# An encoder layer on one core: own buffers for one quarter of x, and another order of products in the first input block

## The chip, the cores and the metric

The kernel runs on one core of one Trainium2 chip. The metric is the device time of one execution in microseconds (us). Below, TensorE is the matrix engine (PE in the profile, PEld its weight loads), VectorE is DVE, ScalarE is ACT, GpSimd is POOL, and SyncE (SP) issues all the DMA transfers spoken of here.

## The reference

One layer of a streaming encoder runs over 2048 prompt tokens and a sample of 8 x 16 tokens, with a model width of 1024. Two groups of heads (an mLSTM with a matrix state, and attention over a sliding window) are fed by one combined input projection. Their results go through an output projection, a LayerNorm, a convolutional feed-forward network and a second LayerNorm. Everything is float32. The part that matters here is the input projection `x @ w_in`:

```python
def trunk_layer(x, pos, C0, n0, m0, k_cache, v_cache, conv_prev, mchunk, w_in, ...):
    qm, km, vm, om, ip, fp, qa, ka, va = split_in(x @ w_in)
    ...
    mix = jnp.concatenate([hm, ha], axis=-1) @ w_out
    h = layer_norm(DEEPNORM_ALPHA * x + mix, ln1_g, ln1_b)
    f, conv_rows = conv_ffn(h, conv_prev, w_up, w_conv, b_conv, w_down)
    y = layer_norm(DEEPNORM_ALPHA * h + f, ln2_g, ln2_b)
```

## The kernel before

**Split numbers.** A float32 operand is split into two parts that TensorE takes: ScalarE casts it to the high half (a 128x1024 cast takes about 1.05 us), VectorE subtracts that from the source and leaves the low half (about 1.2 us). Each product is then three matmuls: high x high, high x low, low x high.

**Blocks and groups.** The input projection goes through four blocks of 512 prompt tokens (`IBLOCKS`; the first block carries the 128 sample tokens as a fifth tile, index 4). In each block five groups g = 0 to 4 of 512 weight columns are computed (g 0 and 1: queries and keys of the mLSTM; 2: queries of the attention; 3 and 4: output gates and values).

**Seven products.** Each group of a block is computed by a scheme of Strassen's kind: x is cut into quarters (xr 1 to 4), the weights too, and seven products s = 1 to 7 of half size replace eight. Product s reads the x combination of the same number. Three PSUM banks A, B, C take them: A takes products 1 and 2; B takes 6, 5 and 3 on top of a copy of A; C takes 7 and 4. `i_after` empties the banks:

- after 6, ScalarE copies B into a tile u2 (L826 calls the copy of L815);
- after 2, A is copied out and stored (`i_out`, L807);
- after 5, ScalarE copies B into u4 (L815) and VectorE adds C to it (L819, or L821 for g of 2 and more); u4 is stored;
- after 4, VectorE adds C to u2 (same lines), and u2 is stored;
- after 3, B is copied out (L807) and refilled with A (L843), where product 1 of the next group stands already.

In the first block the sample's tokens are multiplied along with products 1, 2, 5 and 4 into a bank psx (L758). For g of 0 and 1 they are transposed later (pxt, L875), behind the product that follows 4.

**Direct tiles.** Gates and the keys and values of the attention are not done by the scheme. For each tile of 128 tokens a direct product (item "t", L774) reads two quarters of x as they are. Tiles 0 and 1 of a block read the splits named 1 and 2, tiles 2 and 3 read those named "b12" and 3. The split "b12" is the cast of xr 2, and no product of the scheme reads it. It is written into the buffers of slot 4 (`x_slot(4 if s == "b12" else s)`), which hold the x of product 4 at other times.

**Order.** `i_begin` writes out the order of all items by hand; TensorE runs them in just this order. Block 0 begins with products 1 and 2 of group 0 and 1 of group 1, five direct tiles, then products 7 and 6; then, group by group, 5, 4, 3, 7 and 1 of the next group, 6, 2 and so on. The last group of block 0 ends with 5, 3, 4, and directly behind it come direct tiles 2 and 3 of block 1. In later blocks two direct tiles of the old block stand between the last product and these two. A list `uq` made from the items sets in which order the weights are loaded and split; the splits go through a ring of eight halves, so a split waits until a product has released its buffers. The other engines' instructions and the DMA issues are ordered by a scheduler, by their place in the program and by when it reckons them ready; each engine then works strictly in its order.

**First block's weights.** In block 0 the sums of weight quarters that the scheme needs are made on VectorE in place (`split_first`): for product 7 a11 = a11 - a21 (L528); then a21 = a21 + a22 (L523) and a11 = a22 - a11 (L525), the weight of product 6. For g of 0 and 1 each sum is also stored (`keep`, L521) for the later blocks, and L525 overwrites what the store of product 7's weight reads.

**x's steps.** `x_steps` makes the x combinations: "t3", "t2", "t4", "t1" are VectorE's sums in place (L578, L581, L584, L588), the others are casts (L593 and L594). `begin` says after which item of block 0 the steps of the first block come; `passages` says after which product of a block's last group the steps for the next block come. At the passage from block 0, "b12" comes after product 4. `tc.issue_after(ins)` puts what is issued inside it behind `ins` on the engine of `ins`; it adds no semaphore.

Of the kernel before, what the change touches and what calls it, by code (L numbers as in the profile page):

```python
# [43 lines left out]
NG = 5  # L44
# [160 lines left out]
class Prog:  # L205
# [137 lines left out]
    def i_begin(self):  # L343
        self.ib = [self.dps.tile([P, 512], F32, name="dps", tag="dps") for _ in range(3)]
        it = []
        nb = len(IBLOCKS)
        for b in range(nb):
            if b == 0:
                it += [("p", 0, 0, s) for s in (1, 2)] + [("p", 0, 1, 1)]
                it += [("t", 0, i, -1) for i in (0, 1, 2, 3, 4)] + [("p", 0, 0, s) for s in (7, 6)]  # L350
            else:
                it += [("p", b, 0, s) for s in (1, 7, 6, 2)]
            for g in range(NG):
                if b == 0:

                    it += [("p", b, g, s) for s in (6, 2)] * (g > 0) + [("p", b, g, 5)]
                    if g + 1 < NG:
                        it += [("p", b, g + 1, 1)] * (g > 0) + [("p", b, g, 4), ("p", b, g, 3), ("p", b, g + 1, 7)]
                    else:
                        it += [("p", b, g, 3), ("p", b, g, 4)]  # L360
                elif g + 1 < NG:

                    it += [("p", b, g, s) for s in (6, 7, 2)] * (g > 0)
                    it += [("p", b, g, 5), ("p", b, g + 1, 1), ("p", b, g, 3), ("p", b, g, 4)]
                else:
                    it += [("p", b, g, s) for s in (6, 7, 5, 2, 3, 4)]
            if b:
                it += [("t", b, i, b) for i in (0, 1)]
            if b + 1 < nb:
                it += [("t", b + 1, i, b) for i in (2, 3)]  # L370
        self.items = it

        uq = []
        for i in it:
            if i[0] == "p":
                uq.append(i)
            elif ("g", i[3], 0) not in uq:
                uq += [("g", i[3], u) for u in range(4)]
        uq += [("o", b, h, u) for b in range(len(OBLOCKS)) for h in range(2) for u in range(4)]
        self.uq = uq  # L380
        self.wu, self.hx, self.xr = {}, {}, {}
        self.us = self.ur = 0

        self.halves = [0, 0]
        self.raws = []
        self.raw_of = {}
        self.x_room = {1: [None, False], 7: [None, False]}
        self.xn = self.ny = 0
        self.hs = {}
        self.spare = False  # L390
        self.extra, self.ring, self.turn = None, 2 * WB, 0
        self.raws.append([None, False])
# [177 lines left out]
    def x_steps(self, b, *steps):  # L570

        nc, V = self.nc, self.nc.vector
        r = lambda q: self.xr[b, q]
        for s in steps:
            if s == "t3":
                self.spare = False
                self.xt = e = self.raw_slot([P, 4, HT]) if b else [self.tp.tile([P, 4, HT], F32, name="xt", tag="qk", bufs=2), False]
                V.tensor_sub(e[0], r(4), r(2))  # L578
            elif s == "t2":

                V.tensor_add(self.xt[0], self.xt[0], r(1))  # L581
            elif s == "t4":

                V.tensor_sub(r(4), r(3), self.xt[0])  # L584
                self.xt[1] = True
            elif s == "t1":

                V.tensor_sub(r(2), r(2), r(1))  # L588
            else:
                x = self.xt[0] if s in (7, 6) else r({1: 1, 2: 3, 3: 4, "b12": 2, 5: 2, 4: 4}[s])  # L590

                self.hx[b, s] = h, l = self.x_slot(4 if s == "b12" else s)
                nc.scalar.copy(h, x)  # L593
                V.tensor_sub(l, x, h.bitcast(F32))  # L594

# [17 lines left out]
    def i_dense(self):  # L613
        nc, a = self.nc, self.a
# [17 lines left out]
        for q in (2, 4):  # L632
            for _ in range(2 + (q == 2) * 2):
# [15 lines left out]
                 ("t", 0, 0, -1): ["t2", 6], ("t", 0, 2, -1): ["t1", 5, "t4"]}  # L649
        self.sb, self.trans = {}, None  # L650

        passages = [{1: ["load"], 7: ["t3", 7], 6: ["t2", 6], 3: [3, "t4"], 4: ["b12", "t1"]},
                    {1: ["load"], 6: ["t3"], 7: [7, "t2"], 5: [6], 3: [3, "t4"], 4: ["b12", "t1"]}]
        sums = 0
        after = None
        for item in self.items:
# [9 lines left out]
            if item[0] == "t":  # L666
                _, b, ti, e = item
# [25 lines left out]
            _, b, g, s = item  # L693
# [7 lines left out]
            behind = self.i_after(b, g, s)  # L701
# [4 lines left out]
            if g == last and b + 1 < nb:  # L706
                if s == 7:
                    self.rope_load(IBLOCKS[b + 1][2], 2)
                for x in passages[b > 0].get(s, ()):
                    if x == "load":  # L710
                        self.spare = True
                        self.x_load(b + 1, 1, 2, 3, 4)
                    else:
                        self.x_steps(b + 1, x)
            if (b, g, s) == (0, last, 4):
                self.x_steps(1, 1, 2)
                after = [6, 1]
            if g == last and b + 1 == nb and s in (7, 5, 2, 3):
                self.x_pair(0, (7, 5, 2, 3).index(s))
            with self.tc.issue_after(behind) if behind and b == 0 else nullcontext():  # L720
                self.advance()
                self.x_steps(0, *begin.get(item, ()))
                if item == ("p", 0, 0, 2):
                    self.x_single(4)
# [74 lines left out]
    def i_out(self, b, g, i, j, src):  # L799

        nc = self.nc
        ev = src if i else self.zev()
        if g == 3:
            nc.scalar.activation(ev, src, AF.Tanh, scale=0.5)
            nc.vector.tensor_scalar_add(ev, ev, 1.0)
        elif not i:
            nc.scalar.copy(ev, src)  # L807
        if g == 2:
            self.rope(ev, IBLOCKS[b][2 * j], 2, nc.gpsimd if b > 1 else nc.vector)
        self.i_store(b, g, i, j, ev)  # L810

    def i_after(self, b, g, s):
        nc, V = self.nc, self.nc.vector
        A, B, C = self.ib
        copy = lambda d, x: nc.scalar.activation(d, x, AF.Copy, scale=KSCALE) if g < 2 else nc.scalar.copy(d, x)  # L815

        def add(u):
            if g < 2:
                V.scalar_tensor_tensor(u, C, KSCALE, u, op0=ALU.mult, op1=ALU.add)  # L819
            else:  # L820
                V.tensor_add(u, C, u)  # L821
        if s == 1 and g == 0:
            return nc.scalar.copy(B, A).ins
        elif s == 6:
            self.u2 = self.zev()
            copy(self.u2, B)  # L826
        elif s == 2:
            self.i_out(b, g, 0, 0, A)
        elif s == 5:
            u4 = self.zev()  # L830
            copy(u4, B)
            add(u4)
            self.i_out(b, g, 1, 1, u4)
        elif s == 4:
            add(self.u2)
            self.i_out(b, g, 1, 0, self.u2)
            if b == 0:
                self.i_batch(g)
        elif s == 3:
            self.i_out(b, g, 0, 1, B)  # L840
            if g + 1 < NG:

                nc.scalar.copy(B, A)  # L843
# [1348 lines left out]
```

## Time and profile before

| what | value |
|---|---|
| median of 3 runs | 2310.88 us (2309.37 to 2311.18) |
| the profiled execution | 2311.53 us |
| its span, first to last instruction | 2309.7 us |
| TensorE busy | 2278.2 us (99%) |
| VectorE, ScalarE busy | 1805.2 us (78%), 1305.5 us (57%) |
| DMA moved | 624.98 MB, mean 271 GB/s |
| granted TensorE clock over the span | 0.999 |

The profile tells of one execution. A row of the timeline gives start and duration in us, engine, line of the program, operation, output and inputs, and in brackets how long the engine had been idle and what ended that. A row of the waits gives who waited for whom: us in total, times, longest. A row of the windows gives a stretch, its length, the busy time of PE, PEld, DVE, ACT and POOL in it, the granted TensorE clock, the share of the DMA engines that is busy, and GB/s. A row of the engine groups or DMA issues gives counts and means; for a DMA the KB each and the median us from issue to landing.

### The profile page before, as it was taken

What the parts mean: (1) busy time and instruction counts of PE and PEld (TensorE: products, weight loads), DVE (VectorE), ACT (ScalarE), POOL (GpSimd) and SP (SyncE); (2) the same over time, 40 slices, a digit from 0 to 9 for tenths busy, and PEclk for the clock granted to TensorE, in tenths of its full rate; (3) what the DMA queues carried; (4) which work ended last, traced back from release to release, by engine and by line L of the source; (5) the groups of instructions that cost most, each with busy time, mean ns of one, the idle gap of its engine ahead of it and who ended that gap; (6) DMA issues with size and microseconds to landing.
All of it is one profiled execution on the core that took longest, in us unless ns stands there. A gap on an engine that the chain in (4) does not pass through costs nothing.

```text
span 2309.7 us, 39905 instructions
## 1 busy us (share of the span) xinstructions
PE 2278.2 (99%) x14425; PEld 2099.4 (91%) x14425; DVE 1805.2 (78%) x3157; ACT 1305.5 (57%) x2465; POOL 227.3 (10%) x289
## 2 busy tenths in 40 slices
PE   9999999999999999999999999999999999999998
PEld 8999999999877778999999999999999988888887
DVE  8777587786689888987888667778766787796897
ACT  5453466776766565555556455556555544654653
POOL 0001001001122121200002000002000000000100
PEclk9999999999999999999999999999999999999999
DMA  8898999889976667787777899888998786756753
GB/s 279 300 320 276 302 318 319 293 299 331 302 256 219 219 214 259 272 326 279 281 269 259 278 312 320 311 304 271 331 287 262 243 284 223 244 196 222 245 187 110
DMA packets 297365, 624.98 MB, mean 271 GB/s; under 512 B 47052, under 2 KB 140240, under 8 KB 297168
## 3 DMA queue, kind: packets, MB, share of 16 engines
q1 hardware_dynamic: 296304, 619.29, 78.5%
q10 hardware_dynamic: 864, 3.15, 0.4%
q8 instruction: 114, 1.87, 0.3%
q14 instruction: 83, 0.68, 0.1%
HBM read 451.78 MB, written 170.56 MB: 269 GB/s over the span
## 4 chain that ended last, share of the span: by engine, by line
PE 72%; DVE 6%; DMA 3%; issue 2%; ACT 2%; POOL 0%; SPq 0%; DVEq 0%; ACTq 0%; POOLq 0%
PE dps L1896 18%; PE fup L1896 18%; PE dps L2100 6%; PE dps L749 6%; PE fht L2100 6%; PE fup L2100 5%; PE dps L225 2%; PE dps L227 1%; PE dps L226 1%; PE ppo L1385 1%; PE psc L1336 1%; PE ppt L1379 1%; DVE w L221 1%; DMA wv<-wup 1%; DMA r<-zf 1%
## 5 line engine op out<-in xcount | busy, mean ns | idle before, releaser
L1896 PE MATMUL dps<-hh,uw 128*128 128x384 f32 (+1 forms) x1848 | 477.7, 327 | 5.7 <-DVE u L1929 2.6
L1896 PE MATMUL fup<-hh,uw 128*128 128x384 f32 (+1 forms) x1848 | 476.5, 326 | 0.0
L1944 DVE SCALAR_TENSOR_TENSOR cc<-u,cw,cc 128x768 f32<-128x768 f32 (+1 forms) x264 | 257.6, 977 | 124.9 <-ACT cc L1942 121.5
L1896 PEld LDWEIGHTS dps<-hh,uw 128*128 128x128 f32 x1848 | 329.4, 188 | 8.2 <-DVE u L1929 3.2
L1896 PEld LDWEIGHTS fup<-hh,uw 128*128 128x128 f32 x1848 | 329.4, 188 | 0.0
L1896 PE MATMUL fup<-hl,uw 128*128 128x384 f32 (+1 forms) x924 | 301.3, 326 | 1.0 <-DVE hl L221 1.0
L1896 PE MATMUL dps<-hl,uw 128*128 128x384 f32 (+1 forms) x924 | 301.0, 326 | 0.0
L749 PE MATMUL dps<-w,oh 128*128 128x256 f32 x1344 | 250.2, 282 | 3.6 <-DMA w<-zws 2.1
L749 PEld LDWEIGHTS dps<-w,oh 128*128 128x128 f32 x1344 | 209.2, 188 | 15.9 <-issue 10.5
L220 ACT CAST uw<-wraw 128x1024 fp32r<-128x1024 f32 x126 | 123.2, 981 | 173.4 <-PE dps L2100 104.1
L221 DVE TENSOR_TENSOR w<-wraw,w 128x1024 fp32r<-128x1024 f32 (+1 forms) x155 | 180.8, 1171 | 48.3 <-ACT w L220 46.6
L220 ACT CAST w<-wraw 128x1024 fp32r<-128x1024 f32 (+1 forms) x155 | 155.2, 1008 | 99.8 <-PE dps L749 49.5
L221 DVE TENSOR_TENSOR uw<-wraw,uw 128x1024 fp32r<-128x1024 f32 x126 | 142.4, 1130 | 63.9 <-ACT uw L220 63.8
L749 PE MATMUL dps<-w,ol 128*128 128x256 f32 x672 | 186.2, 277 | 0.0
L1942 ACT ACTIVATE cc<-u,cw 128x768 f32<-128x768 f32 (+1 forms) x132 | 131.9, 999 | 94.6 <-DVE u L1938 91.7
L1896 PEld LDWEIGHTS fup<-hl,uw 128*128 128x128 f32 x924 | 173.5, 188 | 1.8 <-DVE hl L221 1.8
L749 PE MATMUL dps<-oh,w 128*128 128x256 f32 x896 | 170.3, 284 | 4.1 <-ACT zev L807 1.5
L1896 PEld LDWEIGHTS dps<-hl,uw 128*128 128x128 f32 x924 | 173.5, 188 | 0.0
L2100 PE MATMUL fup<-uw,fu 128*128 128x512 f32 x726 | 169.1, 389 | 0.0
L2100 PEld LDWEIGHTS fup<-uw,fu 128*128 128x128 f32 x726 | 136.1, 188 | 28.4 <-ACT fht L2107 0.2
L2100 PE MATMUL dps<-uw,fu 128*128 128x512 f32 x660 | 160.9, 389 | 0.1
L749 PEld LDWEIGHTS dps<-oh,w 128*128 128x128 f32 x896 | 140.4, 188 | 10.4 <-issue 4.1
(346 smaller groups left out, 4596.2 us busy)
## 6 DMA issues: line engine op xcount, KB each, us to landing
uw<-zw SPq DMA_DIRECT2D x176, 512.0 KB, 5.0
zw<-uw SPq DMA_DIRECT2D x88, 512.0 KB, 2.9
w<-zws SPq DMA_DIRECT2D x72, 512.0 KB, 6.2
wv<-wup SPq DMA_DIRECT2D x66, 512.0 KB, 5.8
wraw<-wi SPq DMA_DIRECT2D x62, 512.0 KB, 5.3
wraw<-zt SPq DMA_DIRECT2D x60, 512.0 KB, 4.3
wraw<-wdn SPq DMA_DIRECT2D x45, 512.0 KB, 3.8
wraw<-wo SPq DMA_DIRECT2D x40, 512.0 KB, 4.7
```

The source lines that it names most:

```text
L220: nc.scalar.copy(hi, src)
L221: nc.vector.tensor_sub(lo, src, hi.bitcast(F32))
L225: mm(out, ah, bh, start=start, stop=False)
L226: mm(out, ah, bl, start=False, stop=False)
L227: mm(out, al, bh, start=False, stop=stop)
L749: mm(o, l, r, start=s in (1, 7) and c == k == i == 0, stop=k == 3 and i == 2, skip_group_check=True)
L1336: nc.tensor.matmul(ps[kvh][:, j, :nk], q[rs, j0 + j], k[rs, sel], start=i == 0, stop=i == 2)
L1379: nc.tensor.transpose(pp[:, j * P:(j + 1) * P], scs[j // 2][:, 2 * kvh + j % 2, kt * P:(kt + 1) * P], self.ident)
L1896: mm(ps, l[:, k], r[:, k], start=s in (1, 7) and k == 0 and i == 0, stop=k == 3 and i == 2, skip_group_check=True)
L1942: S.activation(c[:, v], u[:, v, 2:2 + n], AF.Identity, bias=w[3], scale=w[2])
L1944: V.scalar_tensor_tensor(c[:, v], u[:, v, i:i + n], w[i], c[:, v], op0=ALU.mult, op1=ALU.add)
L2100: mm(ps, l[:, k, c], r[:, k], start=s in (1, 4, 7) and u == 0 and k == 0 and i == 0, stop=u == nu - 1 and k == n - 1 and i == 2, skip_grou ...
```

## The change

1. The split "b12" gets two buffers of its own (4 KB per partition each) in place of those of slot 4.
2. At the passage from block 0 to block 1 its cast comes after product 2 of the last group instead of after product 4, and is tied behind the eviction of that product on ScalarE (`i_out` and `i_after` now return that instruction; the tie that existed behind product 1 keeps to product 1).
3. In block 0, group 0 runs 6, 7, 5, 3, 4 instead of 7, 6, 5, 4, 3, and group 1 runs 6, 7, 2 instead of 7 (behind group 0's product 3), 6, 2. The weights of both groups are still split 7 before 6; those of group 0's products 3 and 4 swap with their products.

```diff
--- before.py
+++ after.py
@@ -347,15 +347,17 @@
         for b in range(nb):
             if b == 0:
                 it += [("p", 0, 0, s) for s in (1, 2)] + [("p", 0, 1, 1)]
-                it += [("t", 0, i, -1) for i in (0, 1, 2, 3, 4)] + [("p", 0, 0, s) for s in (7, 6)]
+                it += [("t", 0, i, -1) for i in (0, 1, 2, 3, 4)] + [("p", 0, 0, s) for s in (6, 7)]
             else:
                 it += [("p", b, 0, s) for s in (1, 7, 6, 2)]
             for g in range(NG):
                 if b == 0:
 
-                    it += [("p", b, g, s) for s in (6, 2)] * (g > 0) + [("p", b, g, 5)]
-                    if g + 1 < NG:
-                        it += [("p", b, g + 1, 1)] * (g > 0) + [("p", b, g, 4), ("p", b, g, 3), ("p", b, g + 1, 7)]
+                    it += [("p", b, g, s) for s in ((), (6, 7, 2), (6, 2))[min(g, 2)]] + [("p", b, g, 5)]
+                    if g == 0:
+                        it += [("p", b, g, 3), ("p", b, g, 4)]
+                    elif g + 1 < NG:
+                        it += [("p", b, g + 1, 1), ("p", b, g, 4), ("p", b, g, 3), ("p", b, g + 1, 7)]
                     else:
                         it += [("p", b, g, 3), ("p", b, g, 4)]
                 elif g + 1 < NG:
@@ -376,6 +378,9 @@
                 uq.append(i)
             elif ("g", i[3], 0) not in uq:
                 uq += [("g", i[3], u) for u in range(4)]
+        for g in (0, 1):
+            i, j = [uq.index(("p", 0, g, s)) for s in (6, 7)]
+            uq[i], uq[j] = uq[j], uq[i]
         uq += [("o", b, h, u) for b in range(len(OBLOCKS)) for h in range(2) for u in range(4)]
         self.uq = uq
         self.wu, self.hx, self.xr = {}, {}, {}
@@ -589,7 +594,7 @@
             else:
                 x = self.xt[0] if s in (7, 6) else r({1: 1, 2: 3, 3: 4, "b12": 2, 5: 2, 4: 4}[s])
 
-                self.hx[b, s] = h, l = self.x_slot(4 if s == "b12" else s)
+                self.hx[b, s] = h, l = self.x_slot(s)
                 nc.scalar.copy(h, x)
                 V.tensor_sub(l, x, h.bitcast(F32))
 
@@ -649,7 +654,7 @@
                  ("t", 0, 0, -1): ["t2", 6], ("t", 0, 2, -1): ["t1", 5, "t4"]}
         self.sb, self.trans = {}, None
 
-        passages = [{1: ["load"], 7: ["t3", 7], 6: ["t2", 6], 3: [3, "t4"], 4: ["b12", "t1"]},
+        passages = [{1: ["load"], 7: ["t3", 7], 6: ["t2", 6], 2: ["b12"], 3: [3, "t4"], 4: ["t1"]},
                     {1: ["load"], 6: ["t3"], 7: [7, "t2"], 5: [6], 3: [3, "t4"], 4: ["b12", "t1"]}]
         sums = 0
         after = None
@@ -711,13 +716,14 @@
                         self.spare = True
                         self.x_load(b + 1, 1, 2, 3, 4)
                     else:
-                        self.x_steps(b + 1, x)
+                        with self.tc.issue_after(behind) if x == "b12" and s == 2 else nullcontext():
+                            self.x_steps(b + 1, x)
             if (b, g, s) == (0, last, 4):
                 self.x_steps(1, 1, 2)
                 after = [6, 1]
             if g == last and b + 1 == nb and s in (7, 5, 2, 3):
                 self.x_pair(0, (7, 5, 2, 3).index(s))
-            with self.tc.issue_after(behind) if behind and b == 0 else nullcontext():
+            with self.tc.issue_after(behind) if behind and b == 0 and s == 1 else nullcontext():
                 self.advance()
                 self.x_steps(0, *begin.get(item, ()))
                 if item == ("p", 0, 0, 2):
@@ -800,14 +806,16 @@
 
         nc = self.nc
         ev = src if i else self.zev()
+        done = None
         if g == 3:
             nc.scalar.activation(ev, src, AF.Tanh, scale=0.5)
             nc.vector.tensor_scalar_add(ev, ev, 1.0)
         elif not i:
-            nc.scalar.copy(ev, src)
+            done = nc.scalar.copy(ev, src).ins
         if g == 2:
             self.rope(ev, IBLOCKS[b][2 * j], 2, nc.gpsimd if b > 1 else nc.vector)
         self.i_store(b, g, i, j, ev)
+        return done
 
     def i_after(self, b, g, s):
         nc, V = self.nc, self.nc.vector
@@ -825,7 +833,7 @@
             self.u2 = self.zev()
             copy(self.u2, B)
         elif s == 2:
-            self.i_out(b, g, 0, 0, A)
+            return self.i_out(b, g, 0, 0, A)
         elif s == 5:
             u4 = self.zev()
             copy(u4, B)
```

## The prediction

> **What bounds the kernel now.** I read the totals of the page first, then the list of what TensorE waited for, cut to the first 300 us, because the change touches only the first input block and the hand-over to the second.
>
> ```profile
> span 2309.7 us, 39905 instructions
> PE 2278.2 (99%) x14425; PEld 2099.4 (91%) x14425; DVE 1805.2 (78%) x3157; ACT 1305.5 (57%) x2465; POOL 227.3 (10%) x289
> ...
> PE dps L774 <- DVE ol L594: 2.7, 1, 2.7
> ...
> PE dps L749 <- DVE zev L819: 0.9, 1, 0.9
> ...
> PE dps L749 <- ACT zev L815: 0.7, 1, 0.7
> ```
>
> TensorE is the bound: 2278.2 of 2309.7 us. So the change can only win by removing TensorE's own waits, and every new wait of TensorE costs its full length. The three waits shown, 4.3 us together, are the ones that the change aims at. L774 is the direct tiles' matmul, L749 the seven products', L594 the low half of a cast of x, L815 and L819 the evictions that make "u".
>
> **The large wait: the second block's first direct tile, t(1,2).** The timeline there, by engine:
>
> ```profile
> 150.38 1.58 PE L758 MATMUL psx<-w,xs 128*128 128x256 f32 x12
> 152.35 0.51 PE L774 MATMUL dps<-w,oh 128*128 128x264 f32 x2 [0.40 <-ACT oh L593]
> 155.53 0.39 PE L774 MATMUL dps<-w,ol 128*128 128x264 f32 x1 [2.67 <-DVE ol L594]
> 159.85 0.40 PE L774 MATMUL dps<-w,oh 128*128 128x264 f32 x2
> 162.75 0.28 PE L749 MATMUL dps<-oh,w 128*128 128x256 f32 x1
> ...
> 150.31 1.99 ACT L593 CAST oh<-xr 128x1024 fp32r<-128x1024 f32 x2
> ...
> 151.39 1.23 DVE L594 TENSOR_TENSOR ol<-xr,oh 128x1024 fp32r<-128x1024 f32 x1 [0.20 <-ACT oh L593]
> ...
> 153.13 1.22 DVE L584 TENSOR_TENSOR xr<-xr,wraw 128x1024 f32<-128x1024 f32 x1
> 154.26 1.22 DVE L594 TENSOR_TENSOR ol<-xr,oh 128x1024 fp32r<-128x1024 f32 x1
> ...
> 152.52:155.93 3.41, 0.74 (x5) 0.53 (x6) 3.41 (x5) 1.21 (x2) 0.00 (x0) 1.00 0.76 213
> 155.93:159.34 3.41, 3.41 (x17) 3.41 (x17) 2.30 (x3) 1.04 (x1) 0.00 (x0) 0.50 0.96 347
> ...
> 1575.75:1579.16 3.41, 1.69 (x11) 1.43 (x10) 3.41 (x5) 2.47 (x3) 3.01 (x3) 1.00 0.82 271
> ```
>
> The two casts at 150.31 are x3 and then b12. I know the order because t4 (L584, which overwrites what x3's low half reads) runs at 153.13, after the first L594 and before the second. b12 is written into slot 4, which product (0,4,4) reads until the psx matmuls begin at 150.38; so it is late by its buffer, not by its data. TensorE waits for its high half (0.40), then for its low half, which VectorE finishes at 154.26 + 1.22 = 155.48 (2.67).
>
> A gapless tile takes 162.75 - 159.85 = 2.90 us. The sample matmuls end at 150.38 + 1.58 = 151.96. A tile has 24 matmuls, 0.12 us from one to the next, and groups overlap as two matmuls do: a matmul lasts 0.28, so the next group begins 0.16 before the last one ends. So t(1,2) was due at 151.80 and its successor at 154.70, but the successor begins at 159.85: the hand-over costs 5.15 us. Of it 3.07 are the two waits. In the 3.41 us behind them the granted clock is 0.50: half of 3.41, 1.71 us, is lost once more. The remaining 0.37 is overlap lost at the two restarts.
>
> With its own slot and its place behind the eviction of product (0,4,2), the cast comes here:
>
> ```profile
> 136.29 1.22 DVE L578 TENSOR_TENSOR wraw<-xr 128x1024 f32<-128x1024 f32 x1
> ...
> 149.96 1.23 DVE L221 TENSOR_TENSOR w<-wraw,w 128x1024 fp32r<-128x1024 f32 x1 [2.31 <-ACT w L220]
> ...
> 139.62 0.59 ACT L807 COPY zev<-dps 128x512 f32<-128x512 f32 x1 [0.35 <-PE dps L749]
> ...
> 143.63 0.64 ACT L220 CAST w<-wraw 128x528 fp32r<-128x528 f32 x1 [0.99 <-DMA wraw<-wg]
> 144.17 0.58 ACT L815 COPY zev<-dps 128x512 f32<-128x512 f32 x1
> ```
>
> L807 is that eviction. The source quarter is there: t3 (L578) reads it at 136.29. So the tie adds no wait for data; queued behind the cast on ScalarE are x2's cast, the direct tiles' weight casts and the eviction at 144.17, on which product (0,4,3) waits. The cast, half of the 1.99 us of the two at 150.31, goes into the 0.99 us that ScalarE idles ahead of 143.63, so that eviction is at most some 0.1 us late. VectorE's 1.22 us go into its idle 2.31 us ahead of 149.96. I count both moves at nothing; with that cover gone they would cost TensorE up to the 1.0 us of the cast.
>
> What is late next in that place: x3's cast stays behind the eviction of (0,4,3), and its low half ends at 151.39 + 1.23 = 152.62. t(1,2) needs it from its thirteenth matmul, 151.80 + 12 x 0.12 = 153.25. The slack is 0.63 us, and it shrinks if the added VectorE work delays the release of raw buffers ahead of it. Behind t(1,3), product (1,0,1) writes the bank that the keys' copy of t(1,2) must have emptied; if ScalarE holds x5's cast ahead of that copy, up to about 0.6 us is lost. Bounds for this part: 5.15 at best, 3.9 if both happen. I take 4.9: neither is due by the rows, and a quarter microsecond is for small delays. For blocks 2 and 3 the slot is only freer; I count nothing.
>
> **The two small waits in the first group.**
>
> ```profile
> 36.30:42.12 5.82, 5.81 (x48) 5.61 (x48) 1.00 0.66 187
> ...
> 42.80 0.38 PE L749 MATMUL dps<-oh,w 128*128 128x256 f32 x1 [0.69 <-ACT zev L815]
> 45.74 1.57 PE L758 MATMUL psx<-w,xs 128*128 128x256 f32 x12
> 48.23 0.39 PE L749 MATMUL dps<-oh,w 128*128 128x256 f32 x1 [0.92 <-DVE zev L819]
> 55.67 0.73 PE L875 MATMUL pxt<-ident,zev 128*128 128x128 f32 x4
> 56.16 0.36 PE L749 MATMUL dps<-oh,w 128*128 128x256 f32 x1
> ...
> 45.94 0.60 ACT L815 ACTIVATE zev<-dps 128x512 f32<-128x512 f32 x1 [0.17 <-PE dps L749]
> ...
> 29.62 1.21 DVE L221 TENSOR_TENSOR w<-wraw,w 128x1024 fp32r<-128x1024 f32 x1
> 33.43 1.21 DVE L594 TENSOR_TENSOR ol<-xt,oh 128x1024 fp32r<-128x1024 f32 x1
> ```
>
> Products 7 and 6 take 5.82 us, 2.9 each. Then 5 waits 0.69 for the copy out of bank B that follows 6, and 4 waits 0.92 for the add that reads bank C. In the new order 6, 7, 5, 3, 4 product 7 lies over the first copy. Product 3 adds into bank B, which the copy at 45.94 has left by 46.54, under the sample matmuls that run until 47.31. The add on C then has product 3's 2.9 us. Product 6 may begin at 36.30: its weight's low half is done at 30.83, its x at 34.64. So both waits go: 1.61 us, and 0.16 of overlap regained at each, 1.93.
>
> **What takes it back.** The next group's product (1,6) moves ahead of (1,7), while the weights are still made 7 first, then 6:
>
> ```profile
> 45.28 0.38 SPq L469 DMA_DIRECT2D wraw<-wi  x1
> 45.71 0.43 SPq L521 DMA_DIRECT2D zws<-wraw  x1
> ...
> 52.02 1.23 DVE L525 TENSOR_TENSOR wraw<-wraw 128x1024 f32<-128x1024 f32 x1 [1.26 <-DMA zws<-wraw]
> 54.44 2.36 DVE L221 TENSOR_TENSOR w<-wraw,w 128x1024 fp32r<-128x1024 f32 x2
> ...
> 53.35 2.00 ACT L220 CAST w<-wraw 128x1024 fp32r<-128x1024 f32 x2 [4.40 <-DVE wraw L525]
> 57.21 0.60 ACT L807 COPY zev<-dps 128x512 f32<-128x512 f32 x1
> 57.85 0.57 ACT L843 COPY dps<-dps 128x512 f32<-128x512 f32 x1
> ...
> zws<-wraw SPq DMA_DIRECT2D x5, 512.0 KB, 3.5
> 44.63:52.00 7.37, 6.45 (x55) 6.25 (x54) 5.74 (x19) 1.87 (x3) 0.00 (x0) 1.00 0.97 308
> ```
>
> L525 makes the weight of (1,6) in place and may not begin before the store of the (1,7) weight has read it: issued at 45.71, landed at 52.0. So the high half of (1,6) is there at about 54.4, the low half at about 55.6 (the first of the two at 54.44). None of this hangs on TensorE. Before, (1,6) begins near 56.16 + 2.9 = 59.1 and never sees it. After, the five products and two sample parts, which ended just ahead of the transposes of 55.67, end 1.93 sooner, near 53.65; (1,6) comes straight behind and has all its weights only at 55.6, having done two matmuls (0.25) meanwhile. That gives back about 1.8 of the 1.93. Net for the first groups: 0.1 us won. The bounds are far apart: 1.9 won if the store lands some 2 us sooner, 2.6 lost by the first rival. I take 0.1, because its rows are the nearest.
>
> **The sum.** 4.9 + 0.1 = 5.0 us off the profiled execution, which took 2311.5 us (span 2309.7 and 1.8 around it): 2306.5. The median of the runs was 2310.88, so the prediction is 2305.9. A measurement of this kernel can tell about 0.2%, 4.6 us, from no change: the forecast lies just beyond it.
>
> [...] The half clock came when TensorE had worked 0.74 of a 3.41 us stretch, and did not come at 1.69 of 3.41 (1575.75). [...]
>
> **Rivals.** *The first groups gain in full:* the store of 512 KB landed 6.3 us after its issue, against a median of 3.5 in this stretch, and it stood behind a load of equal size issued at 45.28. One place earlier in the queue, it lands near 49 to 50 and (1,6) doesn't wait: 4.9 + 1.9 = 6.8, 2304.1. For it: SyncE's order is the scheduler's to choose. Against: the queue is full (0.97 of its share). 0.23.
>
> *The first groups lose:* bank B must be emptied and refilled (L807, L843, 1.17 us) before (1,6). If ScalarE keeps those copies behind both casts of 53.35, (1,6) begins at 55.35 + 1.17 = 56.5, 0.9 later than its weights; TensorE has then idled 2.9 us in a row, as long as at 152, and half clock takes 1.7. The loss is 2.6, the sum 2.3 won: 2308.6. 0.13.
>
> *The half clock was not in the runs behind the median, or transfers pulled forward delay the weights by as much:* 3.3 won, 2307.6. For it: the DMA share is 0.96 and 0.95 right behind the wait. Against: the weights there are made some 4 us ahead. 0.12.
>
> *Slower:* the store on which L525 waits lands later still. Now (1,6) stands in front, so each microsecond is one of TensorE's, and 1.7 of half clock come on top. It cancels the gain from 5.0 - 1.7 = 3.3 us later on, and makes the kernel slower by 4.6 from 7.9: more than four further transfers of 512 KB at 308 GB/s (1.7 each) ahead of it. At 9 us later it gives 2310.9 - 5.0 + 1.7 + 9 = 2316.6. Only two such loads stand ahead of it now. 0.06.
>
> **Numbers.** The forecast has 0.46, the rivals 0.23, 0.13, 0.12 and 0.06. The forecast's own range, 3.9 to 6.0 won, lies seven tenths beyond 4.6: 0.32 faster, 0.14 the same. Faster: 0.32 + 0.23 = 0.55. Same: 0.14 + 0.13 + 0.12 = 0.39. Slower: 0.06. The range leaves out the slower case and the edges: from the full gain with half a microsecond of fewer late waits, 2303.3, to just above the losing first groups, 2309.3.
>
> **What would show it.** Right: no wait at L774 for L594 near 147, the granted clock whole there, the next tile 2.9 us later; 5 behind 7 and 3 behind 5 without a wait; a wait of about 2 us of L749 for L221 near 54. Wrong: a wait for the keys' copy or x3 instead; the wait at 54 absent or over 2.5; the gain lost again between 160 and 350, as longer waits for the stored weights.

## The result, and the profile after

| | before | after |
|---|---|---|
| median, both measured side by side | 2311.36 us (10 runs, 2309.37 to 2315.08) | 2318.00 us (10 runs, 2311.40 to 2321.30) |
| the profiled execution | 2311.53 us | 2319.62 us |

The ratio is 1.0021 with a 95% interval of 1.0012 to 1.0029: the change makes the kernel slower by about 0.2%. The forecast was 2305.9 us, with a range of 2303.3 to 2309.3. The page of the changed kernel begins:

```profile
span 2317.8 us, 39910 instructions
...
PE 2282.3 (98%) x14425; PEld 2103.1 (91%) x14425; DVE 1804.4 (78%) x3157; ACT 1303.9 (56%) x2465; POOL 226.9 (10%) x289
```

TensorE runs the same 14425 matmuls. Of the 8.1 us that the span grew, 4.1 are more busy time and 4.0 more waiting. The longer busy time for the same matmuls goes with stretches of half clock, shown below.

In this kernel the lines stand a little lower: L749 is now L755 (products), L758 L764 (sample), L774 L780 (direct tiles), L593/L594 L598/L599 (casts of x), L807 L814, L815 L823, L843 L851 (evictions and refill), L525 L530 (weight of product 6), L894 L902 (a sum of rows, below). All experiments keep the line numbers of before.

**The hand-over won what was forecast.** The timeline after:

```profile
152.25 1.58 PE L764 MATMUL psx<-w,xs 128*128 128x256 f32 x12
153.67 0.40 PE L780 MATMUL dps<-w,oh 128*128 128x264 f32 x2
...
159.48 0.28 PE L755 MATMUL dps<-oh,w 128*128 128x256 f32 x1
...
141.49 0.59 ACT L814 COPY zev<-dps 128x512 f32<-128x512 f32 x1 [0.35 <-PE dps L755]
141.98 1.06 ACT L598 CAST oh<-xr 128x1024 fp32r<-128x1024 f32 x1
...
143.28 1.22 DVE L599 TENSOR_TENSOR ol<-xr,oh 128x1024 fp32r<-128x1024 f32 x1
...
146.17 1.22 DVE L593 TENSOR_TENSOR xr<-xr 128x1024 f32<-128x1024 f32 x1
```

The cast of b12 now comes at 141.98, directly behind the eviction at 141.49, as forecast, and its low half ends at 144.50. It is this cast and not x2's, because t1 (L593), which overwrites the quarter that b12 is made from, runs at 146.17, and 143.28 is the only low half of a quarter that ends before it. The two direct tiles run from 153.67 to 159.48, 2.9 us each, without a wait. From the sample matmuls to product (1,0,1) it was 162.75 - 150.38 = 12.37 us before and is 159.48 - 152.25 = 7.23 now: 5.14 us won.

**The first groups lost 1.4 us.** TensorE reaches the sample matmuls 152.25 - 150.38 = 1.87 us later than before. Of this, 36.78 - 36.30 = 0.48 us was there when the first product in the new order began; the traces of the experiments, too, are 0.2 to 2.4 us later there than the kernel before. So the new order lost 1.39. The timeline where product (1,6) begins:

```profile
55.01 0.39 PE L755 MATMUL dps<-oh,w 128*128 128x256 f32 x1 [0.89 <-ACT w L220]
56.27 0.50 PE L755 MATMUL dps<-oh,w 128*128 128x256 f32 x2 [0.76 <-DVE w L221]
...
53.91 2.94 ACT L220 CAST w<-wraw 128x1024 fp32r<-128x1024 f32 x3 [2.82 <-DVE wraw L530]
...
52.66 1.23 DVE L530 TENSOR_TENSOR wraw<-wraw 128x1024 f32<-128x1024 f32 x1 [1.43 <-DMA zws<-wraw]
...
54.99 2.36 DVE L221 TENSOR_TENSOR w<-wraw,w 128x1024 fp32r<-128x1024 f32 x2
```

It reads as forecast: VectorE may begin L530 only when the store has landed, the high half follows, the low half follows that, and TensorE waits 0.89 + 0.76 us. What the forecast left out is the clock. The stretches of 3.41 us, with the granted clock in the third column from the end:

```profile
56.66:60.07 3.41, 3.41 (x18) 3.41 (x18) 3.41 (x4) 0.75 (x3) 0.00 (x0) 0.50 0.80 287
53.25:56.66 3.41, 1.76 (x13) 1.35 (x12) 3.24 (x9) 2.75 (x3) 0.00 (x0) 1.00 0.72 243
...
322.90:326.31 3.41, 3.41 (x18) 3.41 (x17) 3.20 (x11) 0.97 (x2) 0.32 (x1) 0.50 1.05 359
541.35:544.77 3.42, 3.42 (x18) 3.42 (x17) 0.92 (x3) 2.24 (x7) 0.00 (x0) 0.50 0.89 283
319.49:322.90 3.41, 0.77 (x7) 0.57 (x6) 3.41 (x19) 2.27 (x5) 0.00 (x0) 1.00 0.97 317
537.94:541.35 3.41, 1.03 (x8) 1.03 (x9) 2.31 (x3) 3.41 (x11) 0.00 (x0) 1.00 0.99 378
```

Besides one at the very end of both, before had one such stretch of half clock, at 155.93; after has three, at 56.66, 322.90 and 541.35, each costing half of 3.41 us.

**The rest was lost far from the edit.** At 159.48 TensorE is 3.27 us ahead of before (162.75). At the end it is 8.05 behind. So 11.3 us go in between, 10.2 of them by 600 us, most in the third and fourth input blocks. The two largest places:

```profile
311.79 0.39 SPq L896 DMA_DIRECT2D txy<-wdn  x1
...
317.29 0.69 DVE L902 TENSOR_TENSOR txy<-txy 128x512 f32<-128x512 f32 x1 [2.16 <-DMA txy<-wdn]
...
319.70 0.49 DVE L1196 BATCH_NORM_STATS2 bst<-pnum 128x6 f32<-128x128 f32 x2
...
320.28 0.17 ACT L1199 ACTIVATE mr<-pnum 128x2 f32<-128x2 f32 x1 [3.79 <-DVE bmv L1197]
...
321.84 0.58 ACT L814 COPY zev<-dps 128x512 f32<-128x512 f32 x1
...
322.47 0.38 PE L755 MATMUL dps<-oh,w 128*128 128x256 f32 x1 [2.64 <-ACT zev L814]
...
526.31 0.69 DVE L902 TENSOR_TENSOR txy<-txy 128x512 f32<-128x512 f32 x1 [3.12 <-DMA txy<-wdn]
...
527.75 0.20 ACT L1083 ACTIVATE emt<-col 128x4 f32<-128x4 f32 x1 [3.49 <-DVE col L1078]
...
538.28 0.56 ACT L814 COPY zev<-dps 128x512 f32<-128x512 f32 x1
...
539.69 0.58 ACT L851 COPY dps<-dps 128x512 f32<-128x512 f32 x1
...
540.32 0.39 PE L755 MATMUL dps<-w,oh 128*128 128x256 f32 x1 [2.73 <-ACT dps L851]
```

txy are two tiles into which rows of the down-projection's weights (wdn) are loaded during input blocks three and four; `d_sums` takes four sums of them on VectorE (L902 to L905) and stores them, work that is done ahead for a later stage. At 317.29 VectorE, strictly in its order, has stood 2.16 us waiting for a load issued at 311.79 (L896). The norm's statistics (L1196) stand behind the sums, ScalarE has idled 3.79 us waiting for these, and the eviction that TensorE needs (L814) stands behind that on ScalarE. TensorE waits 2.64 us and gets half clock. For the second place the way from the wait for the rows (526.31) to the late evictions (538.28) was not followed step by step. Before, the wait at the first place was 1.5 us, the longest from 300 to 560 us, and there was no half clock; near 540 us there was no wait at all:

```profile
PE dps L749 <- ACT zev L807: 2.4, 2, 1.5
```

Only reading suggests that the rows are the cause. The experiments test it against other readings.

### The profile page after: what moved, and what is told of

Same layout as the page of the kernel before. It is cut to its first block, busy times and chain, and to the rows that moved or that the text cites. A ratio compares the mean times of both kernels' runs of the same rounds, so it can differ in the third digit from the quotient of the medians.

```text
span 2317.8 us, 39910 instructions
## 1 busy us (share of the span) xinstructions
PE 2282.3 (98%) x14425; PEld 2103.1 (91%) x14425; DVE 1804.4 (78%) x3157; ACT 1303.9 (56%) x2465; POOL 226.9 (10%) x289
## 3 DMA queue, kind: packets, MB, share of 16 engines
q8 instruction: 114, 1.87, 0.3%
## 4 chain that ended last, share of the span: by engine, by line
PE 77%; DVE 9%; DMA 6%; ACT 3%; issue 3%; SPq 1%; POOL 0%; DVEq 0%; ACTq 0%; POOLq 0%
PE dps L1904 18%; PE fup L1904 18%; PE dps L755 11%; PE dps L2108 6%; PE fht L2108 5%; PE fup L2108 5%; DMA txy<-wdn 2%; DVE w L221 2%; PE dps L225 2%; PE dps L227 1%; PE dps L226 1%; PE ppo L1393 1%; PE psx L764 1%; PE dps L780 1%; PE psc L1344 1%
## 5 line engine op out<-in xcount | busy, mean ns | idle before, releaser
L755 PE MATMUL dps<-w,oh 128*128 128x256 f32 x1344 | 252.0, 283 | 6.3 <-ACT dps L851 2.7
L755 PEld LDWEIGHTS dps<-w,oh 128*128 128x128 f32 x1344 | 210.1, 189 | 18.9 <-issue 10.3
L755 PE MATMUL dps<-w,ol 128*128 128x256 f32 x672 | 186.8, 278 | 0.0
L755 PE MATMUL dps<-oh,w 128*128 128x256 f32 x896 | 173.3, 287 | 6.2 <-ACT zev L814 2.6
L755 PEld LDWEIGHTS dps<-oh,w 128*128 128x128 f32 x896 | 142.4, 190 | 13.0 <-issue 4.1
```

The lines of the kernel that those rows point to most:

```text
L755: mm(o, l, r, start=s in (1, 7) and c == k == i == 0, stop=k == 3 and i == 2, skip_group_check=True)
```

## The experiments

Their edits are put together from these pieces:

```diff
 A, own buffers in all four blocks:
-                self.hx[b, s] = h, l = self.x_slot(4 if s == "b12" else s)
+                self.hx[b, s] = h, l = self.x_slot(s)
 A1, only for the second block (A12, A13: b not in (1, 2), (1, 3)):
+                self.hx[b, s] = h, l = self.x_slot(4 if s == "b12" and b != 1 else s)
 T, early tied cast: "b12" after product 2 in the first passage, issued behind that product's eviction
 O, order of products and of their weights in the first two groups, as in the change
```

**1. Which half of the change loses?** One kernel with A and T, one with O alone.

> Only the own buffers for b12 and its early, tied cast; the order of products as before. Theory A (the later blocks' instructions, which the scheduler orders anew once b12 has its own buffers, cost the time): the hand-over at 152 us gains 5.1 us, the first groups are as before, and the waits near 323 us (over 2.5 us) and near 540 us (over 2.5 us), each with a stretch of half clock behind it, are there as in the changed kernel; the time is the changed kernel's less some 2 us, about 2314 to 2317. Theory B (the new order of products in the first groups shifts what follows and so makes the late waits): the late waits are as in the kernel before (1.5 us near 324, none near 540), and the time is about 2306.

> Only the new order of products in the first two groups; b12 shares slot 4 and is cast late, as before. Theory A: the first groups lose 0.4 us without and some 2 us with half clock (product 6 of group 1 waits 1.6 us for its weight), the wait of 3.1 us at the hand-over stays, the late waits are as before: 2311.5 to 2313.5. Theory B: the late waits near 323 and 540 us appear here: 2315 or more.

The buffers and the cast alone: 2317.96 us, ratio 1.0022 (1.0012 to 1.0032), the whole loss. The order alone: 2310.54, 0.9997 (0.9988 to 1.0006), nothing. What TensorE waited for from 30 to 200 us in the kernel with the order alone (us in total, times, longest):

```profile
PE dps L774 <- DVE ol L594: 2.7, 1, 2.7
PE dps L749 <- DVE w L221: 0.8, 1, 0.8
```

The old wait at the hand-over is there, beside the new one of (1,6), here only 0.8 us. And in the other kernel from 300 to 560 us:

```profile
PE dps L749 <- ACT zev L815: 3.1, 2, 2.8
PE dps L749 <- ACT zev L807: 3.1, 1, 3.1
PE dps L749 <- ACT dps L843: 2.8, 1, 2.8
```

So the late waits come with the buffers, not with the order.

**2. Own buffers for the second block alone** (A1 and T), and the same with the first group's new order (6, 7, 5, 3, 4; group 1 in the old one).

> As e1, but only the second block's b12 has its own buffers; the third and fourth blocks' b12 go into slot 4 again, as before. The order of each engine's instructions is then that of the kernel before everywhere but around the hand-over. Theory A: the 5.1 us of the hand-over are kept to the end: 2306 to 2307, the late waits as before. Theory B: no difference from e1. A third theory (C: whatever arrives earlier after the hand-over is lost again to transfers or to half clock, whoever orders the instructions): 2309 to 2311.

> As e6, with group 0 in the new order 6, 7, 5, 3, 4 and group 1 in the old one (product 7 first, then 6). Theory A: both waits of the first group go and product 7 covers the late weight of product 6, so 1.5 to 1.9 us more than e6: 2304 to 2305.5. Theory B: late waits as in the changed kernel, 2309 or more.

The first: 2307.12 us, 0.9971 (0.9961 to 0.9981). Here the forecast's 4.9 us stand alone, and 0.29% of 2311.7 is 6.7 us, with an interval of 4.4 to 9.0 (the medians differ by 4.6). From 300 to 560 us no wait of TensorE is over 1.5 us. In that stretch TensorE loses 12.2 us on the kernel before with A and T, by its place in the two traces, and with A1 and T it gains 0.7. The buffers of the other blocks are what costs. The second: 2307.28, 0.998 (0.9972 to 0.9989), no gain more, and the timeline shows a new wait:

```profile
56.59 0.39 PE L749 MATMUL dps<-oh,w 128*128 128x256 f32 x1 [2.41 <-DVE zev L819]
```

The addition that empties bank C runs only at 55.85: in VectorE's order it stands behind L525 (51.24, 1.23 us) and behind two low halves of weights (53.58, 2.36 us).

**3. The block.** Own buffers for the second and third block (A12 and T), and for the second and fourth (A13 and T).

> As e6, with own buffers for b12 in the second and third blocks; only the fourth block's goes into slot 4. If each block's own buffers bring their own late waits: the waits near 320 and 388 us as in e1, the one near 540 us not; 2312 to 2315. If the third block's buffers alone matter: as e1, 2317 or more. If the fourth block's alone: as e6, 2307.

> Own buffers for the second and the fourth block, the shared buffers of slot 4 for the first and third; early tied cast, old order of products. Second alone took 2307.1 us, second and third 2310.7 (against 2312.8 beside it, so 3.1 to 3.5 above second alone), all blocks 2318.0. If each block's buffers bring their own late waits, the fourth's cost what is left, about 7 us: 2313.5 to 2315, with a wait of 2.4 us or more near 388 or 542 us and half clock behind it. Rival: the late waits need the third block's buffers too (there the third's cast and the fourth's no longer share a pair): 2307 to 2309, no wait above 1.6 us beyond 330 us.

With the third: 2310.65 us, 0.9993 (0.9983 to 1.0004). With the fourth: 2314.19, 1.0008 (0.9999 to 1.0017). Against second alone they add about 0.22% and 0.37%, and the sum, 0.59%, is near the 0.51% between the second alone (0.9971) and all blocks (1.0022). Each of the two blocks brings its own loss; the first block, which shares slot 4 in both kernels, is not needed for it. The loss with the third block is smaller than was expected. The waits agree. With the third, from 300 to 560 us, one wait over 2 us is there, at 321.6:

```profile
PE dps L749 <- ACT zev L807: 3.8, 2, 2.8
```

With the fourth, the wait near 540 us is back, and the one near 320 is 1.5 us:

```profile
PE dps L749 <- ACT zev L807: 2.9, 2, 1.5
PE dps L749 <- ACT dps L843: 2.7, 1, 2.7
```

What moved is seen in VectorE's order in the traces. How many of VectorE's instructions run ahead of each of the eight sets of sums (ahead of L894, or L902):

```
                      third block            fourth block
before                369  421  487  546     798  827  865  911
second and third      384  421  472  499     798  827  865  911
second and fourth     369  421  488  547     750  803  839  880
changed kernel        384  421  472  499     750  803  839  880
```

In a block with own buffers six of the eight sets stand 15 to 48 instructions sooner; the first two of the third block stand 15 later and where they were. Other instructions of VectorE and ScalarE change places as well. Nothing in the edit speaks of any of these: the scheduler, free of the wait for slot 4, orders that block's instructions anew. (The expectation of experiment 6 counts places in another way; its numbers are smaller and stand in no trace.)

**4. The sums on GpSimd.** The first attempt to take VectorE's wait for the rows away: A and T with the four sums moved, and the control with A1 and T.

```diff
-            V.tensor_sub(x[:, l], x[:, r], x[:, l])
+            nc.gpsimd.tensor_sub(x[:, l], x[:, r], x[:, l])
 (and the three after it)
```

> e1 (own buffers for b12 in all later blocks, early cast, products in the old order) with the four subtractions of the down-projection's weight rows (L894 to L897, tile txy) on GpSimd instead of VectorE. In e1 VectorE, which works in its order, stands still for the rows' transfers (4.4 us ahead of 380, 1.8 ahead of 314) just before the late waits of TensorE. Theory D (these subtractions, placed ahead of the chain that ScalarE waits for, carry the transfers' lateness to TensorE): the waits near 320, 388 and 540 us shrink to under 1.6 us each and lose their half clock, the time falls from e1's 2318 to 2305 to 2309. Rival E (ScalarE's own order is at fault, evictions queued behind exponentials): they stay, 2314 or more.

> e6 (own buffers for the second block alone) with the same four subtractions on GpSimd: the control for e8. Theory D: within 2 us of e6, 2305 to 2309, since no long late wait is left there to remove. If the move itself is worth several us in any order, 2303 or less, and e8 then says less.

2322.77 us, 1.0047 (1.0035 to 1.006), and the control 2331.56, 1.0086 (1.0071 to 1.0101). The control lost 1.15% by the move alone, so the pair says nothing on the rows. One sum takes a median of 1.29 to 1.30 us on GpSimd in the control, against 0.67 to 0.69 on VectorE. How that makes 20 us and more was not followed up; the control's granted clock was 0.94 from 240 to 350 us and 0.995 over the whole profiled run, against 0.999 over that of the kernel with A1 and T and the sums on VectorE.

**5. The sums without the rows.** The instructions of the sums stay on VectorE in number and shape, but in the input blocks they work on a tile of zeros that is always there. Left out are the sums themselves: the rows are stored as they were loaded. First with A and T, then with A1 and T.

```diff
-            l, r = slice(0, 512), slice(512, D)
+            l, r, x, y = (slice(0, 512), slice(512, D), x, y) if self.dm is None else (slice(0, 512), slice(0, 512), self.dm, self.dm)
 (self.dm is the 128x512 tile of zeros, and None behind the input blocks)
```

> Own buffers in every block and the early tied cast, old order of products (the kernel that took 2318.0 us), and the four subtractions on the down-projection weight rows in the last two of the four input blocks work on a 128x512 tile of zeros that is always there: the same number, engine and shape of instructions, none of them waiting for the rows. Left out is thereby the sums themselves; the rows are loaded and stored back unsummed. Theory D (VectorE stands in its order behind the transfer of the rows, ScalarE's chain steps and evictions behind VectorE, TensorE behind those): the waits of 2.4 to 3.1 us near 320, 388 and 542 us and their half-clock stretches go, and the time falls by 7 to 10 us, to 2308 to 2311. Rival (the new order of the other instructions on ScalarE and VectorE makes the evictions late, the rows are only seen beside it): the waits stay and the time is 2315 to 2318. If one of the three waits alone goes, 2314.

> Control of the run before: own buffers for the second block alone (the kernel that took 2307.1 us), with the same replacement of the subtractions' operands; the sums are left out in the last two of the four input blocks. There the waits of VectorE for the rows are smaller (about 11 us in all from 285 to 560 us, against 25), and no eviction is late by them beyond 1.5 us. Both theories: 2305.5 to 2308, no change beyond 1.5 us. If it falls as much as the other kernel does (by 5 us or more), the rows cost something everywhere and do not tell the two kernels apart.

2306.46 us, 0.9972 (0.9961 to 0.9983), and the control 2304.05, 0.9962 (0.9948 to 0.9975). Both lie some 1.5 us below the range that was expected. The edit does more than take a wait away. With nothing to wait for, the scheduler sets all eight sets at the head of VectorE's order in both kernels, from 3.3 us on:

```profile
L894 DVE TENSOR_TENSOR dm<-dm x8: 679/683/693, 3.3 to 84.7; 128x512 f32<-128x512 f32 x8
```

(The row gives the shortest, median and longest in ns, and the first and last start in us.) So the third and fourth block lose the sums' own work as well as the wait for the rows, the rows' stores no longer wait for VectorE, and some other instructions change places too. All this is worth 0.50% with own buffers in all blocks and 0.09% in the control. So 0.41 of the 0.51% between these two kernels go when the sums leave these blocks (each ratio is known to about 0.1%, so this to some 0.2). The sums' work alone, which the control loses as well, does not explain it. TensorE's waits from 300 to 560 us with own buffers in all blocks, sums without rows:

```profile
PE dps L749 <- ACT zev L815: 1.3, 2, 0.9
PE dps L749 <- DVE zev L821: 0.8, 1, 0.8
PE dps L749 <- ACT zev L807: 0.4, 1, 0.4
```

None of the three waits of 2.8 us and more is left. That shows that the late waits need the sums in these blocks. The rival, the other instructions' new order, is made unlikely but not excluded, because that order did not stay quite the same.

**6. The sums' place.** A and T with the whole work, and the sums issued behind VectorE's addition that ends product 5 (in the fourth group, where they come after product 2, behind the last addition before it).

```diff
-                    self.d_sums(sums, steps.index(s))
+                    with self.tc.issue_after(self.tie) if s == steps[1] else nullcontext(): self.d_sums(sums, steps.index(s))
 (self.tie is the latest addition on bank C)
```

> Own buffers in every block, early tied cast, old order of products (2318.0 us), and the four subtractions on the down-projection weight rows are issued behind VectorE's addition that ends the product of step 5, the full work kept. In VectorE's order of the kernel at 2318.0 us, the 3rd, 4th, 5th and 6th set of the input blocks' subtractions stand at rows 432, 459, 682, 732; in the kernel with own buffers for the second block alone, at 448, 498, 727, 756; here at 514, 554, 734, 796. Theory D, in the form that the place of the subtractions in VectorE's order is what costs (not a later transfer): VectorE's waits for the rows fall from 25 us (285 to 560 us) to under 8, the waits of 2.4 us and more near 320, 388 and 542 us go, and the time is 2306 to 2310. Rival, later transfers: the rows land as late as before and hold up their buffers, which the next block's x needs as well; then the time stays at 2313 or more.

2313.70 us, 1.0006 (0.9997 to 1.0014). By the number the rival holds (2313 or more). Its mechanism, that VectorE waits for the rows as before, does not. VectorE's waits for the rows from 285 to 560 us, first in the kernel with A and T, then here:

```profile
DVE txy L894 <- DMA txy<-wdn: 13.9, 8, 4.4
DVE txy L895 <- DMA txy<-wdn: 11.1, 7, 4.3
```

```profile
DVE txy L894 <- DMA txy<-wdn: 3.9, 1, 3.9
DVE txy L895 <- DMA txy<-wdn: 0.6, 1, 0.6
```

25.0 us become 4.5, and the three large waits of TensorE go. Where the other run stands at 542.7 us, this one stands at 534.3, 8.4 us ahead. So it is the place of the sums that costs, not a longer transfer: from 285 to 560 us a load of rows took 5.9 us at the median from issue to landing with own buffers everywhere, and 6.2 in the kernel before. But the tie moves other work too, and the lead shrinks to 6.3 us by the end. From 300 to 560 us TensorE now waits here:

```profile
PE dps L774 <- DVE zev L821: 2.1, 1, 2.1
PE dps L749 <- ACT zev L807: 1.4, 1, 1.4
PE dps L749 <- DVE zev L821: 1.4, 1, 1.4
PE dps L749 <- DMA w<-zws: 1.1, 2, 0.7
```

Additions that empty bank C (L821) and stored weights (zws) are late instead.

**7. A faster version, twice.** A1 and T, the first group's new order, and L525 of group 1 issued behind the addition on C that stood behind it in experiment 2; then the same with the tie of experiment 6.

```diff
-            V.tensor_sub(r[a11], r[a22], r[a11])
+            with self.tc.issue_after(self.tie) if g == 1 else nullcontext(): V.tensor_sub(r[a11], r[a22], r[a11])
 (and self.advance() is left out after products 5 and 3 of group 0)
```

> e7 (e6 with group 0 in the order 6, 7, 5, 3, 4, then 7 and 6 of group 1), with L525 of group 1 issued behind the addition that empties bank C for product 7 of group 1. In e7 that addition stood behind L525, which waited for a store, and TensorE waited 2.4 us for it near 56. Expected: that wait under 0.5 us, at most 1 us near 58 for the weight of product 6; 1.0 to 2.0 us less than e6, 2305 to 2306. If the first groups' gain does not reach the end: 2307.

> The fastest version so far (2304.55 us: own buffers for the second block alone, early tied cast, new order of the first group's products, the weight sums of group 1 behind the addition that empties bank C) with the same tie on the row subtractions. Taking the rows' wait away altogether was worth 3.1 us in the kernel with own buffers for the second block (2307.1 to 2304.05), so theory D gives 2301.5 to 2304. Rival: in this kernel the waits for the rows hold up no eviction (VectorE's 11 us of them lie beside TensorE's work), 2304 to 2306; or the stores of the rows, now later, meet the next loads, 2306 or more.

The first: 2304.55 us, 0.9971 (0.9962 to 0.9979), the lowest median of all kernels with the whole work. Its VectorE order shows the cure:

```profile
53.50 0.68 DVE L819 SCALAR_TENSOR_TENSOR zev<-dps,zev 128x512 f32<-128x512 f32 x1
54.10 1.22 DVE L525 TENSOR_TENSOR wraw<-wraw 128x1024 f32<-128x1024 f32 x1
```

The addition runs at 53.50 instead of 55.85, and TensorE has no wait from 50 to 62 us. Beside experiment 2's first kernel (2307.12, but the same ratio to the kernel before, 0.9971) the order's own gain is not told from nothing. The second: 2309.86, 0.9984 (0.9975 to 0.9993), slower than without the tie. The number lies where the second rival put it (2306 or more), and a wait of the kind it names is there: the load of the next rows (L888) waits for the store of the rows before it, 8.2 us in two waits from 500 to 640 us. Whether TensorE's loss comes from that was not followed.

## Why the prediction was wrong

**The hand-over: right.** 4.9 us was forecast, 5.14 measured in the trace. The rival by which the half clock was not in the median is not borne out: own buffers for the second block alone gave 6.7 us (4.4 to 9.0), more than that rival's 3.3. The signs that the forecast named for this place and for the first group came as well.

**The first groups: mechanism right, size off.** TensorE entered them 0.48 us behind and stood 1.46 us ahead at 50 us, so that 5 and 4 no longer wait won 1.94 us (forecast 1.93). The wait of (1,6) for its weight was forecast as 1.8, and 1.65 came. The term missed the half clock behind it, 1.71 us, which the forecast had only in the rivals "the first groups lose" and "slower". The first of these expected evictions behind casts; the evictions were on time, and it was the weight itself. Forecast was 0.1 us won; in the profiled run 1.94 won and 1.65 + 1.71 lost leave a loss of 1.42, and its trace shows 1.39. With the order alone the wait was 0.8 us, and from 36 us on TensorE won 1.2 us by 60 us, about what 1.94 - 0.8 leaves without half clock; 0.8 of it were left at 146. That is less than the medians can tell.

**The step that failed** is the sentence "For blocks 2 and 3 the slot is only freer; I count nothing." It took a freed dependency for one that can only help. The slot was freer, and no wait at TensorE hung on it in the third and fourth block, so nothing could be won there. But the scheduler used the freedom to set most of `d_sums`, with other instructions, up to 48 instructions sooner in VectorE's order, ahead of its loads' landing. The term counted at nothing cost about 0.41% by experiment 5, some 9.5 us (known to about 5): more than the hand-over gave. That the late waits need these sums, and come with the third and the fourth block's buffers, is shown; that VectorE's wait for the loads alone makes them, and not the order of its neighbours too, is argued from experiments 5 and 6 together. No rival had this; "slower" was put on a late store in the first groups, which came only in time (1.65 us) and not 7.9 us later.

**Its signs:** the forecast named "the gain lost again between 160 and 350" as a sign against it. The loss came from 160 on and up to 550, most of it behind 320, but not as longer waits for stored weights (from 160 to 600 us these were 2.1 us before and 1.8 after); it came with evictions behind a VectorE that waited.

**A clue that stood in the trace of before.** VectorE's waits from 285 to 560 us, in the kernel before and in the changed one:

```profile
DVE txy L894 <- DMA txy<-wdn: 10.9, 6, 4.0
DVE txy L895 <- DMA txy<-wdn: 2.0, 3, 1.0
```

```profile
DVE txy L902 <- DMA txy<-wdn: 15.1, 7, 4.4
DVE txy L903 <- DMA txy<-wdn: 7.9, 6, 3.0
```

Already before, VectorE stood up to 4.0 us in front of these rows, while TensorE's longest wait there was 1.5 us. That list, read for each block that the edit reaches, could have suggested the rival that was missing.

**Still open:** why the sums go sooner in the scheduler's reckoning; of the 11.3 us lost in the profiled run, the two places shown (with their half clocks) account for 2.69 + 4.56 = 7.25 by the position of TensorE before and behind them, and the rest lies in many small waits that were not followed one by one.

## What to carry to other kernels

Giving an operand its own buffer takes a dependency away in every iteration, also where nothing waited for it. If a scheduler orders the other engines, apply the edit only where a wait goes (here the second block alone was faster, 0.9971, all blocks slower, 1.0022), and compare the instruction order elsewhere. Here an instruction that waited for a transfer held up what stood behind it on its engine: VectorE stood 2.16 us before the sum at 317.29, ScalarE idled 3.79 us ahead of 320.28 until VectorE was done, and TensorE 2.64 ahead of 322.47 until ScalarE was. So look in the trace of before at the bound engine's helpers for long waits that happen to be harmless. Such an instruction belongs behind the work that empties the banks, though a tie that moves it moves others with it, and has to be tried in place.

## What the runs showed of the hardware

- Waits of 0.89 and 0.76 us, 1.65 together, in one stretch of 3.41 us (53.25, TensorE busy 1.76) were followed by half clock (granted 0.50) in the next (56.66). The kernel before had whole clock (1.00) behind a wait of 1.72 us in one stretch (1575.75, busy 1.69). So the busy time of the records, whose ends are modelled, does not alone tell the two cases apart. In the changed kernel the waits of 2.64 us (in the stretch from 319.49, busy 0.77) and 2.73 us (most of it in the stretch from 537.94, busy 1.03) were each followed by one stretch of half clock, too. Its three stretches of half clock are 3.41 us long in the trace and begin at 56.66, 322.90 and 541.35. They lie 266.24 and 218.45 us apart, 78 and 64 times 3.413.
- Waits of similar length, 3.12 and 2.67 us, went with different amounts of half clock. In the kernel with A and T, TensorE idled 2.29 us of the stretch from 316.03 to 319.44 (busy 1.12 of 3.41) and 0.83 of the next (busy 2.58); two stretches of half clock, 319.44 to 326.27, 6.83 us, go with it. In the kernel before, the wait of 2.67 us at the hand-over lay in one stretch (152.52 to 155.93, busy 0.74) and one stretch of half clock, 3.41 us, followed. Whether the place of a wait or its length makes the difference was not shown.
- One subtraction of two 128x512 float32 operands took 1.29 us on GpSimd and 0.69 on VectorE. Moving eleven sets of four there from VectorE made the control slower by 1.15%, and the kernel with A and T by 0.25%.
